# Decay of two tokens from one masked F32 tile, and score tiles placed first in their pool

## The chip, the core and the metric

The kernel runs on one core of a Trainium2 chip. A core has a matrix engine (TensorE, PE in the profile, with its weight loads as PEld), VectorE (DVE), ScalarE (ACT), GpSimd (POOL) and a queue that issues transfers (SyncE, SP). Matrix products write to PSUM, which has eight banks; everything else works on the on-chip memory SBUF, 128 partitions wide. The metric is the device time of one execution in microseconds (us); lower is better. Engines run in parallel and meet only at semaphores, and each engine takes its own instructions in program order.

## What is computed

One layer of a hybrid encoder on 1024 tokens of width 1024, in float32: a mixer made of windowed attention and a bidirectional gated delta rule, then cross-attention into 256 memory tokens, then a gated feed-forward layer. The change lies in the delta rule. For each direction and head, with g the running sum of the per-token log decay, it needs for all pairs of tokens of a chunk

```python
g = jnp.cumsum(g.reshape(b, h, n, c), axis=-1)
incl = jnp.tril(jnp.ones((c, c), dtype=bool))
decay = jnp.exp(jnp.where(incl, g[..., :, None] - g[..., None, :], -jnp.inf))
lower = jnp.where(strict, jnp.einsum('bhnid,bhnjd->bhnij', kb, k) * decay, 0.0)
sol = lax.linalg.triangular_solve(tmat, rhs, left_side=True, lower=True, unit_diagonal=True)
qk = jnp.einsum('bhnid,bhnjd->bhnij', q, k) * decay
```

The second half of the mixer's work that matters here is the windowed attention: scores of a block of 128 tokens against itself and its neighbours, a softmax with a sink, and the product with the values.

## The kernel before, in words

The kernel works in chunks of 128 tokens, eight in all. Matrix products that must be precise in float32 are made of two faster ones: an operand x is split into a high part, x rounded to the type F32R, and a low part, the rest (`split`, L99 to L106), and products of the parts are added in PSUM. A product of two plain F32 tiles is also possible; the kernel uses it for small ones.

The mixer runs in three stretches, each written as a list of steps (ORDER_1 to ORDER_3, L36 to L38), but the order in which an engine issues its instructions is not the order of that list: a scheduler works out every engine's order from the program's dependences and priorities when the kernel is built. Any edit can therefore move instructions that it does not name.

Stretch one, ORDER_1. For each of four heads, D projects and convolves k, q and v (`proj`, products L259; `conv`, four VectorE steps per tile, L284), and P prepares (`prep`, L431): it makes the decay of all token pairs, E; transposes k, q and v (L441), norms them (sums on ACT, L463; rs on POOL, L159 and L160; the product kv on VectorE, L466), transposes back (L473), forms k with k and q with k (L481), and multiplies both with E (U at L484, pc at L488). B inverts the 32x32 diagonal blocks of two heads at a time (`base_inverse`, L498) on VectorE (L515 to L528), with A at L529 on POOL; V and A then go to DRAM (d_inv, L533). B0 serves heads 0 and 1, called group 0, B1 heads 2 and 3, group 1.

E is the exponential of a sum that PE forms in PSUM. With a mask tile mi (ones where token s is at or before token t, or after it for the other direction) times the log decays G of one head, and a triangular matrix ml as the other operand, one product gives the decay sum of every pair of tokens of four chunks at once. G is first split: `ghr` is G cast to F32R, `ghi` its value and `glo` the rest (L352 to L357). For each head, half of the sequence and direction, POOL makes one masked tile `gm` of the high part and one of the low part, and PE adds the four products of both directions in one PSUM bank (L445 to L452). The masked tiles rotate through two buffers, so POOL writes the third when PE has read the first.

Stretch two, ORDER_2. L (`levels`, L536) builds the inverse of each head's whole chunk from the diagonal blocks: it fetches them from d_inv into cz and cw (L544), rearranges them (m5, c5, c6 at L554 to L557; D and Z at L567), masks the transposed U (L5, L6 at L575 and L576), and runs two levels of products (L583 and L589), whose results Z (L605, L606) go to DRAM. G, A and V project the gate, the attention's q and k with their rotary products (sn and rop, L724 and L725), and the values; the values are transposed (L741) and split into `vhl` (L743). W runs the attention windows (`window`, L612), which write their scores into tiles `sc`. Stretch three, ORDER_3, runs the recurrent scan over chunks (L777) with the rest of the windows and the projections of the memory; then the merge product (L1005) begins.

Memory is handed out by pools, which are laid on a stack in the order in which they open. A pool that opens after another closed takes over its memory, and the first instruction that writes a tile there waits until every reader and writer of the old tiles on that spot is done, transfers included. Between stretches one and two the pools of `base_inverse` (tb) and of `prep` (t2) close, and the pool of the windows (tw, L712) opens on the same spot. In a pool each tag's buffers are laid out when it is first asked for; the first here is vhl, 9,216 bytes a partition, and the eight score tiles of 1,536 bytes come later. The inverse's pool held V and A of 4,096 bytes, two small tiles of 128 and tmpb of 1,024.

Of the kernel before, what the change touches and what calls it, by code (L numbers as in the profile page):

```python
# [10 lines left out]
F32 = mybir.dt.float32  # L11
F32R = mybir.dt.float32r
I32 = mybir.dt.int32
AF = mybir.ActivationFunctionType
ALU = mybir.AluOpType
# [4 lines left out]
P = 128  # L20
# [3 lines left out]
NT = S // P  # L24
# [51 lines left out]
def tile_hybrid_block(  # L76
# [6 lines left out]
    nc = tc.nc  # L83
# [9 lines left out]
    def f32(ap):  # L93
        return ap.bitcast(F32)

    def bc(ap, axis, shape):
        return ap.unsqueeze(axis).to_broadcast(list(shape))
# [10 lines left out]
    def pool(name, bufs, **kw):  # L108
        return tc.tile_pool(name=name, bufs=bufs, reuse_waits="tile", **kw)
# [27 lines left out]
    sm = p12.enter_context(pool("sm", 1))  # L137
    C0, C1 = _AT["mUi"], _AT["mU"]
    C = sm.tile([P, C1 - C0], F32, name="C")
    mU_r = sm.tile([P, P], F32R, name="mU_r")  # L140
    mL_r = sm.tile([P, P], F32R, name="mL_r")
    prm = sm.tile([P, 24], F32, name="prm")
    nega = sm.tile([P, 8], F32, name="nega")
    p1 = ExitStack()
# [8 lines left out]
    cm = {n: (C[:, a - C0:a - C0 + P] if a < C1 else CE[:, a - C1:a - C1 + P]) for n, a in _AT.items() if n != "ident"}  # L153
    rope_f, rope_s = (CE[:, _ROPE_AT - C1 + i:_ROPE_AT - C1 + i + 1] for i in range(2))

    def rstd_of(rs, ss, n, eps):

        w = ss.shape[-1]
        nc.gpsimd.tensor_scalar(rs, ss, n, eps, ALU.mult, ALU.add)  # L159
        nc.gpsimd.tensor_tensor(rs, rs, mhalf[:, :w], ALU.pow)  # L160
# [33 lines left out]
    t1 = pa1.enter_context(pool("t1a", 2, side="right"))  # L194

    def small():
        return ps.tile([P, 512], F32, tag="ps", name="ps")
# [11 lines left out]
    for hf in range(2):  # L209
        hi = hx.tile([P, KT, HALF], F32R, name=f"hhi{hf}")  # L210
        lo = hx.tile([P, KT, HALF], F32R, name=f"hlo{hf}")
        for j in range(4):
# [10 lines left out]
            for kq in range(2):  # L223
                pt = small()
                for k in range(4):
                    c = (4 * kq + k) * P
# [15 lines left out]
    nc.scalar.copy(cols, pt[:, :P])  # L242
    nc.sync.dma_start(CE, consts[:, C1:])
    nc.sync.dma_start(C, consts[:, C0:C1])
    nc.vector.tensor_copy(mU_r, cm["mU"])
    nc.vector.tensor_copy(mL_r, cm["mL"])

    nc.sync.dma_start(prm[:, 0:8], a_log[0].rearrange("d h -> (d h)").partition_broadcast(P))
    nc.sync.dma_start(prm[:, 8:16], dt_bias[0].rearrange("d h -> (d h)").partition_broadcast(P))
# [21 lines left out]
    t2 = pp_.enter_context(pool("t2", 2))  # L271
# [28 lines left out]
    t1 = pa1.enter_context(pool("t1b", 1, side="right"))  # L300
# [8 lines left out]
    for hf in range(2):  # L309
        pp = pg.tile([P, 512], F32, tag="pg", name="pg")  # L310
        for k in range(KT):
            for a in range(2):
                nc.tensor.matmul(pp, wabr[:, k, :], hT[hf][a][:, k, :], start=(k == 0 and a == 0),
                                 stop=(k == KT - 1 and a == 1))
# [27 lines left out]
    G = sm.tile([P, 2, 4, NT], F32, name="G")  # L342
# [6 lines left out]
    dump("G", G)  # L349
    dump("beta", beta)  # L350

    ghi = sm.tile([P, 2, 4, NT], F32, name="ghi")  # L352
    glo = sm.tile([P, 2, 4, NT], F32, name="glo")
    ghr = t1.tile([P, 2, 4, NT], F32R, tag="ghr", name="ghr")
    nc.vector.tensor_copy(ghr, G)
    nc.vector.tensor_copy(ghi, f32(ghr))
    nc.vector.tensor_tensor(glo, G, ghi, ALU.subtract)  # L357

    pt = small()
    pv = pt[:, 0:192].rearrange("p (s d n) -> p s d n", s=3, d=2)  # L360
# [54 lines left out]
    def together(gens):  # L415

        gens = list(gens)
        while gens:
            gens = [g for g in gens if next(g, g) is not g]
# [3 lines left out]
    def save(after=None):  # L423

        while unsaved:
            with ExitStack() as order_:
                if after:
                    order_.enter_context(tc.issue_after(after.ins))
                nc.sync.dma_start(*unsaved.pop(0))

    def prep(h, kc, qc, vc):  # L431

        g, hh = h // 2, h % 2
        def part(b):
            c4 = slice(4 * b, 4 * b + 4)

            def turned(src):
                p_ = small()
                for j in range(4):
                    o = (4 * b + j) * P  # L440
                    nc.tensor.transpose(p_[:, j * P:(j + 1) * P], src[:, o:o + P], ident)  # L441
                return p_.rearrange("p (c n) -> p c n", c=4)


            pa = small()  # L445
            n = 0
            for d, (mi, ml) in enumerate((("mUi", mL_r), ("mLi", mU_r))):
                for part in (ghi, glo):
                    gm = t2.tile([P, 4, P], F32R, tag="gm", name="gm")
                    nc.gpsimd.tensor_tensor(gm, bc(part[:, d, h, c4], 2, (P, 4, P)), bc(cm[mi], 1, (P, 4, P)), ALU.mult)  # L450
                    nc.tensor.matmul(pa, ml, gm.rearrange("p c n -> p (c n)"), start=(n == 0), stop=(n == 3))
                    n += 1  # L452
            E = t2.tile([P, 4, P], F32, tag="E", name="E")
            nc.scalar.activation(E, pa.rearrange("p (c n) -> p c n", c=4), AF.Exp)

            kv = t2.tile([P, 4, 4, P], F32, tag="kv", name="kv")
            for src, i, n, e in ((kc, 0, 1.0, EPS), (qc, 3, float(P), P * EPS)):
                yield
                pk = turned(src)
                ss = t2.tile([P, 4], F32, tag="ss4", name="ss4", bufs=4)  # L460
                for j in range(4):
                    jk = t2.tile([P, P], F32, tag="jk", name="jk")
                    nc.scalar.activation(jk, pk[:, j, :], AF.Square, accum_out=ss[:, j:j + 1])  # L463
                rs = t2.tile([P, 4], F32, tag="rs4", name="rs4", bufs=4)
                rstd_of(rs, ss, n, e)
                nc.vector.tensor_tensor(kv[:, :, i, :], pk, bc(rs, 2, (P, 4, P)), ALU.mult)  # L466
            yield
            nc.scalar.copy(kv[:, :, 1, :], turned(vc))
            for i, o in ((0, 2), (3, 3)):
                yield  # L470
                p_ = small()
                for j in range(4):
                    nc.tensor.transpose(p_[:, j * P:(j + 1) * P], kv[:, j, i, :], ident)  # L473
                nc.scalar.copy(kv[:, :, o, :], p_.rearrange("p (c n) -> p c n", c=4))
            nc.sync.dma_start(d_kv[g][c4, :, hh].rearrange("c p s n -> p c s n"), kv)

            for i in (2, 3):
                yield
                p_ = small().rearrange("p (c n) -> p c n", c=4)
                for j in range(4):  # L480
                    nc.tensor.matmul(p_[:, j, :], kv[:, j, 2, :], kv[:, j, i, :], start=True, stop=True)  # L481
                if i == 2:
                    U = t2.tile([P, 4, P], F32, tag="U", name="U")
                    nc.vector.tensor_tensor(U, p_, E, ALU.mult)  # L484
                    nc.sync.dma_start(d_u[g][hh, c4].rearrange("c p n -> p c n"), U)
                else:
                    pc = t2.tile([P, 4, P], F32, tag="pc", name="pc")
                    nc.vector.tensor_tensor(pc, p_, E, ALU.mult)  # L488
                    for d, mi in enumerate(("mUi", "mLi")):
                        pm = t2.tile([P, 4, P], F32, tag="pm", name="pm", bufs=3)  # L490
                        nc.gpsimd.tensor_tensor(pm, pc, bc(cm[mi], 1, (P, 4, P)), ALU.mult)
                        unsaved.append((d_pz[g][d][c4, :, hh, 0].rearrange("c p n -> p c n"), pm))
            if h < 3:
                save()

        together([part(b) for b in range(2)])

    def base_inverse(g):  # L498
# [211 lines left out]
    pw = p12.enter_context(pool("pw", 2, space=PSUM, side="right"))  # L710
    ps = pgs.enter_context(pool("psl", 2, space=PSUM))
    tw = p12.enter_context(pool("tw", 2))  # L712
    vhl = tw.tile([P, NT + 1, 2, 2, 64], F32R, tag="vhl", name="vhl", bufs=1)[:, 0:NT]
    tl_ = p1.enter_context(pool("tl", 2))

# [437 lines left out]
    for k in range(HK):  # L1153
        p0, p1 = turned_k(xn, k), turned_k(xn, k + HK)
        g0, g1 = gain("ffn", k), gain("ffn", k + HK)
        x12, t1, t2_, t3_ = (tr.tile([P, HALF], F32, name=f"r{i}", tag=f"r{i}") for i in range(4))
# [352 lines left out]
```

## Time and profile before

| | us |
|---|---|
| median of 3 runs | 1587.42 |
| lowest and highest run | 1584.72, 1590.94 |
| the profiled execution, its own time | 1588.8 |
| its span, first to last instruction | 1587.1 |
| mean granted PE clock in it | 0.988 |

The profile is of one execution. Its page gives busy time by engine, the span in slices, and the chain of work that ended last, followed back from the end. The trace behind it can be asked for windows of time, for the waits of one engine, for a tile, or for the instructions in order of time. A row of the last kind reads: start in us from the span's start, duration, engine, line, operation, output<-inputs, shape, count, and in brackets how long the engine stood idle just before and which work released it. Matrix products are pipelined: the duration of one is a latency, and what it costs the engine is the distance to the next start.

### The profile page before, as it was taken

How to read it: one execution, taken by the hardware profiler on the slowest of the kernel's cores; microseconds unless marked ns; L12 is line 12 of the kernel's file. 1: busy time of each engine (PE TensorE's matmuls, PEld its weight loads, DVE VectorE, ACT ScalarE, POOL GpSimd, SP SyncE). 2: the span in 40 equal slices, each digit the busy share in tenths (PEclk: the TensorE clock that was granted, in tenths of full speed). 3: DMA queues.
4: the chain of work that ended last, by engine and by line, in shares of the span. 5: the costliest groups of instructions: out<-in, count | busy, mean ns of one | idle time of the engine just before them, and what ended most of it. 6: DMA issues, size and time to landing. Idle time of an engine off the chain costs nothing.

```text
span 1587.1 us, 21186 instructions
## 1 busy us (share of the span) xinstructions
PE 1505.9 (95%) x7514; PEld 1260.3 (79%) x7514; DVE 1059.3 (67%) x1616; ACT 762.4 (48%) x1523; POOL 497.4 (31%) x447
## 2 busy tenths in 40 slices
PE   6999889989799989999999999999999999999998
PEld 5877777868689967788888777888888888888786
DVE  6846887975678865444345549677768655596565
ACT  6556543238766685554335566322322332344532
POOL 2368644233134510243301140443434433100021
PEclk9999999989999999999999999999999999999999
DMA  6134148483998675455222254443335332853354
GB/s 207 42 118 129 41 153 226 113 206 103 283 289 284 191 251 206 146 186 157 69 72 79 90 186 140 128 154 127 118 118 166 100 100 100 292 206 112 107 171 161
DMA packets 252151, 242.97 MB, mean 153 GB/s; under 512 B 33528, under 2 KB 187021, under 8 KB 252045
## 3 DMA queue, kind: packets, MB, share of 16 engines
q1 hardware_dynamic: 252045, 241.62, 48.0%
q8 instruction: 59, 0.97, 0.3%
q14 instruction: 47, 0.39, 0.1%
HBM read 172.07 MB, written 66.88 MB: 151 GB/s over the span
## 4 chain that ended last, share of the span: by engine, by line
PE 67%; DVE 13%; DMA 7%; ACT 5%; issue 3%; POOL 3%; SPq 2%; DVEq 0%; POOLq 0%; ACTq 0%
PE pmg L1005 8%; PE pD L1180 7%; PE pE L1180 7%; PE pA L1180 6%; PE pcq L259 6%; PE pdX L1370 5%; PE pg L259 4%; PE pdA L1370 4%; PE pB L1180 4%; PE psc L777 3%; DVE acc L284 2%; PE pdD L1370 2%; DVE tmpb L524 2%; DVE A L526 2%; PE pcs L1086 1%
## 5 line engine op out<-in xcount | busy, mean ns | idle before, releaser
L102 ACT CAST whi<-wraw 128x1024 fp32r<-128x1024 f32 x108 | 113.3, 1050 | 161.5 <-PE pmg L1005 34.9
L103 POOL TENSOR_TENSOR wlo<-wraw,whi 128x1024 fp32r<-128x1024 f32 x48 | 119.7, 2494 | 193.9 <-ACT whi L102 171.4
L259 PE MATMUL pg<-hlo,whi 128*128 128x512 f32 x352 | 140.2, 399 | 0.0
L259 PE MATMUL pg<-hhi,whi 128*128 128x512 f32 x352 | 140.1, 399 | 0.1
L259 PE MATMUL pg<-hhi,wlo 128*128 128x512 f32 x352 | 139.9, 398 | 0.0
L103 DVE TENSOR_TENSOR wlo<-wraw,whi 128x1024 fp32r<-128x1024 f32 x60 | 74.5, 1244 | 79.4 <-ACT whi L102 75.1
L1005 PE MATMUL pmg<-whi,b 128*128 128x512 f32 x384 | 118.4, 394 | 2.6 <-ACT whi L102 2.2
L1180 PE MATMUL pA<-s,whi 128*128 128x512 f32 x352 | 109.6, 392 | 1.4 <-ACT m L1197 1.4
L284 DVE SCALAR_TENSOR_TENSOR acc<-cp,cols,acc 128x1024 f32<-128x1024 f32 x48 | 73.8, 1539 | 19.5 <-ACT acc L282 18.9
L1005 PEld LDWEIGHTS pmg<-whi,b 128*128 128x128 f32 x384 | 71.2, 188 | 17.9 <-ACT whi L102 2.7
L259 PEld LDWEIGHTS pg<-hhi,whi 128*128 128x128 f32 x352 | 67.1, 191 | 13.6 <-ACT hhi L102 0.4
L1257 POOL TENSOR_TENSOR act<-act,up 128x512 f32<-128x512 f32 x33 | 50.1, 1519 | 88.1 <-DVE up L1256 53.0
L259 PEld LDWEIGHTS pg<-hhi,wlo 128*128 128x128 f32 x352 | 67.1, 191 | 13.2
L259 PEld LDWEIGHTS pg<-hlo,whi 128*128 128x128 f32 x352 | 67.2, 191 | 13.1
L1370 PE MATMUL pdX<-dhl,whi 128*128 128x512 f32 x264 | 76.1, 390 | 1.5 <-ACT dhl L102 0.8
L1180 PEld LDWEIGHTS pA<-s,whi 128*128 128x128 f32 x352 | 65.3, 188 | 15.2 <-ACT m L1197 2.0
L1400 POOL TENSOR_SCALAR frs<-sq 128x1 f32<-128x1 f32 x8 | 11.9, 1497 | 195.7 <-ACT jk L1389 194.8
L1005 PE MATMUL pmg<-wlo,b 128*128 128x512 f32 x192 | 71.4, 391 | 0.0
L1180 PE MATMUL pA<-s,wlo 128*128 128x512 f32 x176 | 68.8, 392 | 1.9 <-DVE wlo L103 1.9
L102 ACT CAST whi<-araw 128x1024 fp32r<-128x1024 f32 (+1 forms) x36 | 35.4, 982 | 71.3 <-PE pdX L1370 27.6
L1229 POOL TENSOR_TENSOR sr<-wraw 128x512 f32<-128x512 f32 x22 | 29.2, 1328 | 126.4 <-DMA wraw<-in_w_gate_up_dram 125.6
L103 DVE TENSOR_TENSOR wlo<-araw,whi 128x1024 fp32r<-128x1024 f32 (+1 forms) x36 | 40.7, 1132 | 38.5 <-ACT whi L102 38.3
(409 smaller groups left out, 4230.3 us busy)
## 6 DMA issues: line engine op xcount, KB each, us to landing
wraw<-in_w_gate_up_dram SPq DMA_DIRECT2D x52, 512.0 KB, 3.9
kv<-d_kv SPq DMA_DIRECT2D x32, 512.0 KB, 6.7
wraw<-in_w_in_dram SPq DMA_DIRECT2D x22, 512.0 KB, 4.3
b<-in_w_down_dram SPq DMA_DIRECT2D x20, 512.0 KB, 7.0
araw<-d_as SPq DMA_DIRECT2D x20, 512.0 KB, 3.7
d_kv<-kv SPq DMA_DIRECT2D x8, 1024.0 KB, 7.2
pz<-d_pz SPq DMA_DIRECT2D x32, 256.0 KB, 6.0
wraw<-in_w_ckv_dram SPq DMA_DIRECT2D x16, 512.0 KB, 7.2
```

What stands on the lines that cost most here:

```text
L102: nc.scalar.copy(hi, src)
L103: (eng or nc.vector).tensor_tensor(lo, src, f32(hi), ALU.subtract)
L259: nc.tensor.matmul(p_, w[:, k, :], ah[a][:, k, :], start=(k == 0 and i == 0), stop=(k == nk - 1 and i == 2))
L284: nc.vector.scalar_tensor_tensor(acc, cp[:, t:t + S], taps[t], acc, ALU.mult, ALU.add)
L524: nc.vector.tensor_tensor(tv, A[:, j + 1:, j:j + 1].to_broadcast([P, n, j]), A[:, j:j + 1, 0:j].to_broadcast([P, n, j]), ALU.mult)
L526: nc.vector.tensor_tensor(A[:, j + 1:, 0:j], A[:, j + 1:, 0:j], tv, ALU.add)
L777: nc.tensor.matmul(out[:, d, h, :], lt[:, d, h, :], rt[:, d, h, :], start=True, stop=True)
L1005: nc.tensor.matmul(pp[t], act[a][:, k, tt], w_[:, kk, :], start=(k == 0 and i == 0), stop=(k == KT - 1 and i == 2))
L1180: nc.tensor.matmul(out_, w[a][:, k, :], xx[b_][:, k, :], start=(start and k == 0 and i == 0), stop=(k == HK - 1 and i == 2), skip_group_ch ...
L1229: nc.gpsimd.tensor_tensor(s[0], b_[:, 0:HK], b_[:, HK:], ALU.add)
L1257: nc.gpsimd.tensor_tensor(o_, o_, up, ALU.mult)
L1370: nc.tensor.matmul(banks[t], a[:, k - k0, tt], w, start=(first and k == 0 and i == 0), stop=(k == NB - 1 and i == 2), skip_group_check=not ...
```

## The change

The split of G into ghr, ghi and glo is gone. For each direction one masked tile of G itself is made, in F32, and one product in F32 is added; the two triangular operands are kept as F32 copies, mU_s and mL_s, instead of F32R ones. So a head needs four masked tiles and four products where it needed eight of each. And in the pool of the windows a score tile is asked for first, so that the eight buffers of that tag are laid at the pool's start, ahead of vhl; the tile that this line returns is not used.

```diff
-    mU_r = sm.tile([P, P], F32R, name="mU_r")
-    mL_r = sm.tile([P, P], F32R, name="mL_r")
+    mU_s = sm.tile([P, P], F32, name="mU_s")
+    mL_s = sm.tile([P, P], F32, name="mL_s")
...
-    nc.vector.tensor_copy(mU_r, cm["mU"])
-    nc.vector.tensor_copy(mL_r, cm["mL"])
+    nc.vector.tensor_copy(mU_s, cm["mU"])
+    nc.vector.tensor_copy(mL_s, cm["mL"])
...
-    ghi = sm.tile([P, 2, 4, NT], F32, name="ghi")
-    glo = sm.tile([P, 2, 4, NT], F32, name="glo")
-    ghr = t1.tile([P, 2, 4, NT], F32R, tag="ghr", name="ghr")
-    nc.vector.tensor_copy(ghr, G)
-    nc.vector.tensor_copy(ghi, f32(ghr))
-    nc.vector.tensor_tensor(glo, G, ghi, ALU.subtract)
...
-            n = 0
-            for d, (mi, ml) in enumerate((("mUi", mL_r), ("mLi", mU_r))):
-                for part in (ghi, glo):
-                    gm = t2.tile([P, 4, P], F32R, tag="gm", name="gm")
-                    nc.gpsimd.tensor_tensor(gm, bc(part[:, d, h, c4], 2, (P, 4, P)), bc(cm[mi], 1, (P, 4, P)), ALU.mult)
-                    nc.tensor.matmul(pa, ml, gm.rearrange("p c n -> p (c n)"), start=(n == 0), stop=(n == 3))
-                    n += 1
+            for d, (mi, ml) in enumerate((("mUi", mL_s), ("mLi", mU_s))):
+                gm = t2.tile([P, 4, P], F32, tag="gm", name="gm")
+                nc.gpsimd.tensor_tensor(gm, bc(G[:, d, h, c4], 2, (P, 4, P)), bc(cm[mi], 1, (P, 4, P)), ALU.mult)
+                nc.tensor.matmul(pa, ml, gm.rearrange("p c n -> p (c n)"), start=(d == 0), stop=(d == 1))
...
     tw = p12.enter_context(pool("tw", 2))
+    tw.tile([P, 384], F32, tag="sc", name="sc", bufs=8)
     vhl = tw.tile([P, NT + 1, 2, 2, 64], F32R, tag="vhl", name="vhl", bufs=1)[:, 0:NT]
```

## The prediction, made before the result was known

> **What bounds the kernel now.** I read the page's busy shares and its chain first.
>
> ```profile
> span 1587.1 us, 21186 instructions
> PE 1505.9 (95%) x7514; PEld 1260.3 (79%) x7514; DVE 1059.3 (67%) x1616; ACT 762.4 (48%) x1523; POOL 497.4 (31%) x447
> PE 67%; DVE 13%; DMA 7%; ACT 5%; issue 3%; POOL 3%; SPq 2%; DVEq 0%; POOLq 0%; ACTq 0%
> ```
>
> PE is busy for 95% of the span and is two thirds of the chain. POOL, which loses most work in this change, is 3% of the chain. Such averages decide nothing for one stage, so next come windows of 20 us over the mixer. Columns: window, its length, busy time of PE, PEld, DVE, ACT, POOL, then granted clock, DMA share, GB/s.
>
> ```profile
> 140.00:160.00 20.00, 19.25 (x109) 16.37 (x108) 10.09 (x11) 7.99 (x13) 12.21 (x14) 1.00 0.67 204
> 180.00:200.00 20.00, 15.38 (x78) 12.65 (x77) 19.52 (x32) 14.74 (x44) 10.50 (x13) 0.91 0.11 30
> 220.00:240.00 20.00, 15.58 (x78) 12.70 (x77) 14.66 (x22) 13.23 (x43) 9.60 (x12) 0.93 0.43 107
> 320.00:340.00 20.00, 14.43 (x72) 11.59 (x71) 15.51 (x18) 6.30 (x14) 9.93 (x7) 0.99 0.90 211
> 340.00:360.00 20.00, 18.16 (x90) 16.27 (x91) 16.18 (x38) 9.77 (x23) 5.64 (x5) 0.75 0.70 185
> 360.00:380.00 20.00, 20.00 (x119) 17.69 (x119) 12.39 (x28) 16.23 (x39) 10.36 (x8) 1.00 0.52 158
> ```
>
> PE is full in 140:160 and 360:380 and stands for about 5 us in each of 180:200, 220:240 and 320:340; in 340:360 it also has three quarters of its clock. So the mixer is PE's work plus a few holes. The view of waits says who dug them (PE, first 640 us; total, times, longest).
>
> ```profile
> PE ps L441 <- DVE kv L466: 5.5, 3, 2.6
> PE ps L583 <- DVE L L576: 5.0, 1, 5.0
> PE ps L473 <- DVE kv L466: 3.8, 3, 1.7
> PE ps L451 <- POOL gm L450: 2.9, 3, 1.5
> PE ps L574 <- DVE Z L606: 2.4, 1, 2.4
> PE ps L441 <- ACT E L454: 2.0, 1, 2.0
> ```
>
> Two families: four lines around the decay (L451, E, and the kv that waits for rs in POOL's queue), 14.2 us in sum, and two in the levels of head 2 (L574, L583), 7.4 us. The change touches both. From the merge product (L1005) on, the two built programs issue the same order on every engine, so the whole effect lies ahead of it and shifts the rest.
>
> **Term 1, PE passes: a loss.** The 32 F32R products of L451 become 16 F32 products of the same 128x512 shape.
>
> ```profile
> L451 PE MATMUL ps<-gm,mL_r x16: 387/395/499, 71.1 to 221.8; 128*128 128x512 f32 x16
> 33.56 13.85 PE pg L259 x61
> 529.34 1.79 PE psc L777 x16
> L777 PE MATMUL psc<-kv,pz 128*128 128x128 f32 x128 | 19.1, 284 | 2.3 <-DMA pz<-d_pz 2.0 <-DVE kv L798 0.3
> ```
>
> The 395 ns is latency; what PE pays is the step in the chain: 61 F32R products of 512 columns in 13.85 us, 0.227 each, so 32 cost 7.3 us. Of F32 the trace has only narrow ones. L777 issues 64 such products with kv and pz (4 per call, 8 steps, 2 groups) and leaves 128 records, two per product, while L451 in F32R leaves one (16 for mL_r). A record of 128 columns steps at 1.79/16 = 0.112. If columns scale, one F32 product of 512 columns is 2 x 4 x 0.112 = 0.90 and 16 are 14.3, a loss of 7.0 us. If each record is no dearer than an F32R one, 32 records cost 7.3 and the loss is 0. I take 7.0: the F32 row is the nearest in kind.
>
> The Trainium skill, "FP8 and Floating Point Precision", section TensorE Precision Notes, speaks against the change: true FP32 takes four passes through the array. By it 16 products are 64 passes of 0.227, 14.5 us, a loss of 7.2; no row of before shows a wide F32 product.
>
> Where these 7 us lie: in the new order the decay does not push the chain back, since 642 projection matmuls stand ahead of the last product of head 3 (L481) where 673 stood, and 895 where 935 stood ahead of the first L583 of head 2. The 40 deferred ones (9.1 us) come later, in a stretch like 360:380 where PE has no hole. So the loss is paid at the end of the projections, before the scan.
>
> **Term 2, fewer masks on POOL: a gain.** Sixteen of 32 gm go, and three 128x64 VectorE steps (the dearest 0.82).
>
> ```profile
> L450 POOL TENSOR_TENSOR gm<-ghi,C x16: 1033/1120/2023, 68.2 to 226.8; 128x512 fp32r<-128x512 f32 x16
> L450 POOL TENSOR_TENSOR gm<-glo,C x16: 1034/1089/2089, 69.4 to 227.8; 128x512 fp32r<-128x512 f32 x16
> 68.46 0.82 DVE L357 TENSOR_TENSOR glo<-G,ghi 128x64 f32<-128x64 f32 x1
> 227.87 0.50 PE L451 MATMUL ps<-gm,mU_r 128*128 128x512 f32 x1 [1.54 <-POOL gm L450]
> 229.19 2.12 DVE L528 TENSOR_TENSOR V<-A,bB 128x1024 f32<-128x1024 f32 x1
> 231.39 2.75 POOL L529 TENSOR_TENSOR A<-A,bB 128x1024 f32<-128x1024 f32 x1 [2.58 <-DVE V L528]
> 235.81 0.69 DVE L466 TENSOR_TENSOR kv<-ps,rs 128x512 f32<-128x512 f32 x1 [3.45 <-POOL rs L160]
> 236.65 0.63 PE L441 MATMUL ps<-ident,acc 128*128 128x128 f32 x4 [2.54 <-DVE kv L466]
> ```
>
> At a median of 1.1 us that is 17.6 us of POOL time, nearly all beside PE work and worth nothing there. On PE's path it can be worth from 0 to the 14.2 us of the four waits. I take half of the 2.9 (gm) and 2.0 (E), since each tile has half as many masks before it, and a quarter of the 9.3 (kv): its rs stands in POOL's queue behind gm at some heads, and at head 3 behind A of the inverse, which stays. Together 2.5 + 2.3 = 4.8, say 5.
>
> **Term 3, score tiles first: a gain.** Before, the first tile of its pool, vhl (9,216 bytes a partition), lies on the memory of the inverse's V and A. With eight score tiles in front (12,288 bytes, the inverse's pool had 9,472) it lies on tiles of the decay stage, long free, and both vhl copies lose their DMA waits. The score tiles inherit the old memory, but are first written by the windows, after those stores.
>
> ```profile
> 288.68 0.28 PE L741 MATMUL ptv<-ident,vT 128*128 128x128 f32 x1
> 317.73 2.04 DVE L528 TENSOR_TENSOR V<-A,bB 128x1024 f32<-128x1024 f32 x1
> 322.23 1.18 SPq L533 DMA_DIRECT2D d_inv<-A  x2
> 326.42 1.07 ACT L102 CAST vhl<-ptv 128x512 fp32r<-128x512 f32 x2 [10.07 <-DMA d_inv<-A]
> 327.05 1.29 DVE L103 TENSOR_TENSOR vhl<-ptv,vhl 128x512 fp32r<-128x512 f32 x2 [4.20 <-ACT vhl L102]
> 328.33 0.65 ACT L605 ACTIVATE Z<-ps 64x256 f32<-64x256 f32 x2
> 330.23 1.09 PE L574 MATMUL ps<-ident,Ul 128*128 128x128 f32 x8 [2.37 <-DVE Z L606]
> 331.75 4.18 DVE L555 COPY c<-cw 32x256 f32<-32x256 f32 x4
> 341.84 3.59 PE L583 MATMUL ps<-m,L 128*128 128x32 f32 x16 [5.04 <-DVE L L576]
> 358.92 1.73 PE ps L583 x16
> ```
>
> The data of vhl are ready at 289; ACT holds it until A has landed, 10.07 us of idle time. Behind it stand khi and the two Z copies (L605) that free the two PSUM banks PE needs for L574, and VectorE idles 4.20 us; its c, D and L steps then end late and PE waits again at L583. In the new order the Z copies stand ahead of vhl on both engines, so the 2.37 goes. What stands ahead of vhl instead is a c copy that waits for a cw fetch, which follows V's store, not A's; behind it wait vhl, khi and the next weight cast. On SP that fetch waits for V's store and the stores of A and of Z queue behind it. So the start of head 2's levels still hangs on the inverse: of the 5.04 I take the 4.20 that VectorE idled. After the hole 16 records of L583 took 3.59 instead of 1.73, and the window had clock 0.75, a loss of at most 0.25 x 20 = 5.0; I take 1.5. Term 3: 2.4 + 4.2 + 1.5 = 8.1; bounds 0 and 2.4 + 5.0 + 5.0 = 12.4.
>
> **Sum.** +7.0 - 4.8 - 8.1 = -5.9. The profiled execution took 1588.8 us (span 1587.1), 1.4 over the median of 1587.42, so 1582.9 for it and 1581.5 for the median.
>
> **Rivals.** One, *the holes swallow the passes*: the F32 records run where PE stands anyway, and term 1 costs nothing. For: PE has some 5 us of hole in each of three windows. Against: the deferred projections fall into full windows. -12.9, 1574.5; with all of term 3's bound, about 1570.
>
> Two, *the wait moves*: ACT stands as long at the c copy as it stood at vhl, because V's store and fetch in SP's queue come no sooner. Term 3 is 0: +7.0 - 4.8 = +2.2, 1589.6. For: nothing shortens the inverse itself. Against: VectorE reaches its start with 22 weight splits and no rotary products ahead where 23 and 4 stood.
>
> Three, slower, *head 3's masks behind the inverse of group 0*: the new POOL order puts A<-A,bB ahead of the last two masks of head 3, which stood ahead of it. PE takes L451 in order, so the projections behind it wait for V, A (2.75) and two masks (2.2): a hole of 5.0, and everything of head 3 and group 1 starts later, which eats terms 2 and 3. +7.0 + 5.0 = +12.0, 1599.4. It decides where V ends after PE has come to these masks; before, PE came at 227.87 and V began at 229.19, so it is close. Against it: 44 convolution steps stand ahead of that V where 48 stood:
>
> ```profile
> L284 DVE SCALAR_TENSOR_TENSOR acc<-cp,cols,acc 128x1024 f32<-128x1024 f32 x48 | 73.8, 1539 | 19.5 <-ACT acc L282 18.9
> ```
>
> Four of 1.539 us are 6.2 us earlier.
>
> **Chances.** Forecast 0.42 (its own range 1575 to 1588), rival one 0.20, two 0.18, three 0.20. The range goes from rival one with most of its bound to three: 1566 to 1600. A measurement of this kernel tells about 0.5%, 8 us, from no change, so faster means under 1579.5: rival one and half of the forecast, 0.41. Slower means over 1595.4: rival three and a tail of two, 0.22. The rest, 0.37, is within.
>
> **What would show it.** Right: L451 in 32 records whose step is near 0.45; vhl with no DMA as releaser and well before the inverse's A lands; no 2.4 us hole at L574, a smaller one at the first L583 of head 2; the scan's first product some 6 us earlier than here:
>
> ```profile
> 408.51 1.20 PE L777 MATMUL psc<-kv,pz 128*128 128x128 f32 x4 [1.97 <-DMA pz<-d_pz]
> ```
>
> Wrong: L451 records stepping at 0.23 (term 1 too dear); ACT idle about 10 us at the c copy before vhl (two); a hole over 4 us at L451 near 225 with POOL's A as cause (three). A first scan product later than this row would make the sum's sign wrong.

## The result, and the profile after

The changed kernel took 1589.53 us in the median of 20 runs (1586.75 to 1595.8), the kernel before 1587.01 us in as many beside it. The ratio is 1.0020, 95% interval 1.0012 to 1.0028: about 3 us slower, where the forecast had it 6 us faster. The difference is below the 8 us that the forecast called "within", but the whole interval lies above 1. The page of the profiled execution:

```profile
span 1587.5 us, 21156 instructions
PE 1511.1 (95%) x7514; PEld 1258.4 (79%) x7514; DVE 1058.5 (67%) x1613; ACT 756.2 (48%) x1519; POOL 466.5 (29%) x431
```

PE is busy 5.2 us longer than before, POOL 31 us shorter, and the span is the same within what one execution tells.

In the changed kernel L441 is L435 and L451 is L443; lines from 454 to about 704 are 9 lower (L574 is L565, L583 is L574, L528 is L519), and later ones 8 (L777 is L769). First the products of the decay, from the view of one line (count, shortest/median/longest in ns, first and last start) and from the timeline:

```profile
L443 PE MATMUL ps<-gm,mL_s x16: 590/591/1203, 71.3 to 223.3; 128*128 128x512 f32 x16
L443 PE MATMUL ps<-gm,mU_s x16: 592/592/1062, 72.2 to 225.7; 128*128 128x512 f32 x16
160.51 1.02 PE L443 MATMUL ps<-gm,mL_s 128*128 128x512 f32 x2
161.37 1.02 PE L443 MATMUL ps<-gm,mU_s 128*128 128x512 f32 x2
```

Sixteen products leave 32 records. Two records start 0.86 us ahead of the next two, so a product costs 0.86, not 0.90, and sixteen cost 13.8: 6.5 more than the 7.3 of before. By the Trainium skill, "FP8 and Floating Point Precision", section TensorE Precision Notes, true FP32 takes four passes; 64 passes of 0.227 make an estimate of 14.5 us, and the trace agrees within 5%.

The waits of PE in the first 640 us (total, times, longest):

```profile
PE ps L435 <- ACT E L445: 5.4, 3, 3.8
PE ps L574 <- DVE L L567: 4.2, 4, 1.8
PE ps L443 <- POOL gm L442: 4.1, 1, 4.1
PE ps L464 <- DVE kv L457: 3.7, 7, 1.1
PE ps L574 <- ACT m L545: 3.6, 1, 3.6
PE ps L565 <- DVE Z L597: 1.9, 1, 1.9
```

The four lines around the decay stood at 14.2 us and are now three with 5.4 + 4.1 + 3.7 = 13.2. The levels stood at 7.4; now the L583 wait of 5.0 in one piece is 4.2 in four, the 2.4 is 1.9, and a new one of 3.6 behind ACT's copy m has come: 9.7. In the same windows as before:

```profile
140.00:160.00 20.00, 20.00 (x106) 17.17 (x105) 10.30 (x9) 6.70 (x9) 8.88 (x8) 1.00 0.76 235
180.00:200.00 20.00, 19.11 (x106) 16.31 (x107) 18.18 (x31) 11.68 (x35) 7.75 (x10) 0.91 0.47 159
220.00:240.00 20.00, 15.53 (x72) 11.05 (x73) 9.51 (x9) 13.19 (x44) 9.04 (x11) 0.91 0.48 110
320.00:340.00 20.00, 16.42 (x75) 13.79 (x74) 15.84 (x20) 5.89 (x11) 8.59 (x6) 0.88 0.88 213
340.00:360.00 20.00, 20.00 (x115) 17.62 (x114) 14.12 (x33) 11.80 (x32) 5.72 (x7) 0.95 0.65 155
360.00:380.00 20.00, 17.55 (x87) 14.69 (x86) 12.70 (x25) 9.21 (x23) 11.02 (x9) 0.91 0.62 186
```

The hole in 180:200 has nearly closed, 320:340 has 2 us more of PE at a lower clock (0.88 for 0.99), and 340:360 is full at 0.95 where it had 0.75. But 220:240 is no better, and 360:380, which was full, now has a hole of 2.5. Head 3's masks show where 220:240 went (POOL, then PE):

```profile
217.54 2.74 POOL L520 TENSOR_TENSOR A<-A,bB 128x1024 f32<-128x1024 f32 x1 [5.19 <-DVE V L519]
220.24 4.00 POOL L442 TENSOR_TENSOR gm<-G,C 128x512 f32<-128x512 f32 x2
222.31 2.06 PE L443 MATMUL ps<-gm,mL_s 128*128 128x512 f32 x2 [4.13 <-POOL gm L442]
```

A of the inverse stands ahead of the two masks, and PE waits 4.13 us for the first of them: the mechanism of rival three. Then the levels of head 2, on ACT, on SP's queue and on PE:

```profile
322.84 0.40 ACT L548 COPY c<-cw 64x256 f32<-64x256 f32 x1 [5.58 <-DMA cw<-d_inv]
323.26 1.07 ACT L102 CAST vhl<-ptv 128x512 fp32r<-128x512 f32 x2
331.93 0.82 ACT L545 COPY m<-cz 32x256 f32<-32x256 f32 x2 [5.57 <-DMA cz<-d_inv]
```

```profile
320.22 1.26 SPq L524 DMA_DIRECT2D d_inv<-A  x2
321.57 3.92 SPq L599 DMA_DIRECT2D d_pz<-Z  x4
325.58 3.44 SPq L721 DMA_DIRECT2D rot<-sn  x4
329.06 0.58 SPq L535 DMA_DIRECT2D cz<-d_inv  x1
```

```profile
334.58 3.27 PE L574 MATMUL ps<-m,L 128*128 128x32 f32 x16 [3.58 <-ACT m L545]
411.12 1.06 PE L769 MATMUL psc<-kv,pz 128*128 128x128 f32 x4
```

The copy to vhl no longer waits for a DMA. But ACT idles 5.58 us at the c copy ahead of it and 5.57 at the m copy behind it, 11.2 in sum where it idled 10.07 once. The fetch of cz stands in SP's queue behind four stores and four rotary copies and leaves at 329.06; before, it left 3.2 us sooner though V ended 3 us later (319.77 against 316.67):

```profile
325.87 0.53 SPq L544 DMA_DIRECT2D cz<-d_inv  x1
```

The scan's first product came at 411.12, 2.6 us later than before: the row that the forecast named for a wrong sign. The delay does not last in these two traces, though. The first merge product (L1005, now L997) starts at 600.51 where before it started at 602.90, and the spans differ by 0.4 us. The 3 us are those of the medians; one execution of each kernel does not show where they arise.

### The profile page after: what moved, and what is told of

It reads as the page before. It is cut to its first block, busy times and chain, and to the rows that moved or that the text cites. A ratio compares the mean times of both kernels' runs of the same rounds, so it can differ in the third digit from the quotient of the medians.

```text
span 1587.5 us, 21156 instructions
## 1 busy us (share of the span) xinstructions
PE 1511.1 (95%) x7514; PEld 1258.4 (79%) x7514; DVE 1058.5 (67%) x1613; ACT 756.2 (48%) x1519; POOL 466.5 (29%) x431
## 5 line engine op out<-in xcount | busy, mean ns | idle before, releaser
L997 PE MATMUL pmg<-whi,b 128*128 128x512 f32 x384 | 118.4, 394 | 2.6 <-ACT whi L102 2.2
L997 PEld LDWEIGHTS pmg<-whi,b 128*128 128x128 f32 x384 | 71.2, 188 | 17.9 <-ACT whi L102 2.7
L284 DVE SCALAR_TENSOR_TENSOR acc<-cp,cols,acc 128x1024 f32<-128x1024 f32 x48 | 77.5, 1616 | 9.4 <-ACT acc L282 8.5
L259 PEld LDWEIGHTS pg<-hlo,whi 128*128 128x128 f32 x352 | 67.4, 192 | 13.7 <-issue 1.0
L997 PE MATMUL pmg<-wlo,b 128*128 128x512 f32 x192 | 71.4, 391 | 0.0
```

What stands on the lines that cost most here:

```text
L259: nc.tensor.matmul(p_, w[:, k, :], ah[a][:, k, :], start=(k == 0 and i == 0), stop=(k == nk - 1 and i == 2))
L284: nc.vector.scalar_tensor_tensor(acc, cp[:, t:t + S], taps[t], acc, ALU.mult, ALU.add)
L997: nc.tensor.matmul(pp[t], act[a][:, k, tt], w_[:, kk, :], start=(k == 0 and i == 0), stop=(k == KT - 1 and i == 2))
```

## The experiments

Each ratio is to the kernel before, run beside it on the same chip; medians are of 5 to 20 runs. Differences between two runs are given in us of 1587, and their uncertainties are estimates from the two intervals.

| run | median us | ratio | 95% interval |
|---|---|---|---|
| changed kernel | 1589.53 | 1.0020 | 1.0012 to 1.0028 |
| p1_f32_alone | 1590.83 | 1.0029 | 1.0016 to 1.0042 |
| p2_sc_first_alone | 1587.21 | 0.9998 | 0.9990 to 1.0007 |
| r16_one_tile_f32r | 1581.69 | 0.9966 | 0.9955 to 0.9978 |
| f32_32_products | 1600.14 | 1.0078 | 1.0066 to 1.0090 |
| gm4_four_masks | 1596.36 | 1.0060 | 1.0045 to 1.0076 |
| zf_fetch_ahead | 1590.47 | 1.0026 | 1.0014 to 1.0039 |
| zg_both | 1599.27 | 1.0079 | 1.0062 to 1.0097 |
| pzg_both_hi_lo | 1599.33 | 1.0077 | 1.0059 to 1.0094 |
| am_masks_then_A | 1593.26 | 1.0032 | 1.0019 to 1.0045 |
| m16_masks_halved | 1585.40 | 0.9987 | 0.9977 to 0.9997 |
| r16n_no_score_tile | 1584.63 | 0.9986 | 0.9974 to 0.9997 |
| i15_half_inverse | 1584.24 | 0.9983 | 0.9972 to 0.9994 |

Two things are read from the traces first. Three pairs issue the same instructions in the same order on every engine, and differ in the placement alone: the kernel before and p2_sc_first_alone, p1_f32_alone and the changed kernel, r16n_no_score_tile and r16_one_tile_f32r. The edits of the decay, in type, number of masks or buffers, move instructions on every engine within the first 150 us, so what they cost or return includes another order. And where the order is the same up to the second inverse, its V ends at 316.67 in the changed kernel, at 318.92 in p1_f32_alone and at 319.71 in zf_fetch_ahead: start times of single traces tell nothing below some 3 us.

**The two parts alone.** First the changed kernel without its score-tile line.

```diff
-    tw.tile([P, 384], F32, tag="sc", name="sc", bufs=8)
```

> The F32 tile alone: the decay from one masked tile in F32, vhl left where it lay in the kernel before. Theory (each part has its own sign): the passes add 16 x 2 x 0.45 - 32 x 0.227 = 7.1 us of PE work, and up to 320 us the changed kernel had the same lost PE time as before (45.3 against 45.2), so the mixer's decay stage gives nothing back: +7 us against before, ratio 1.0044, with ACT still standing about 10 us at vhl for A. Rival one (the passes run in holes): ratio 1.000 +- 0.001. Rival two (all of the 2.5 us by which the changed kernel is slower come from this part, the placement does nothing): +2.5 us, ratio 1.0016.

Measured 1.0029, +4.6 us: between the theory's +7, which lies outside the interval, and the second rival's +2.5 at its edge. This is terms 1 and 2 without term 3. The part on ACT did not come:

```profile
324.89 0.40 ACT L548 COPY c<-cw 64x256 f32<-64x256 f32 x1 [4.32 <-DMA cw<-d_inv]
327.50 1.07 ACT L102 CAST vhl<-ptv 128x512 fp32r<-128x512 f32 x2 [2.21 <-DMA d_inv<-A]
334.38 0.82 ACT L545 COPY m<-cz 32x256 f32<-32x256 f32 x2 [3.77 <-DMA cz<-d_inv]
```

With the order of the changed decay the c copy stands ahead of vhl and waits for the same inverse, so vhl itself waits only 2.21 us, and the placement has no more than that to take there. The changed kernel, which is this run with the placement, is 1.4 us faster, uncertain by 2.4. Then the kernel before with the score-tile line and nothing else.

```diff
+    tw.tile([P, 384], F32, tag="sc", name="sc", bufs=8)
     vhl = tw.tile([P, NT + 1, 2, 2, 64], F32R, tag="vhl", ...
```

> The placement alone: score tiles first in their pool, the decay left in high and low parts in F32R. Theory (each part has its own sign): the lost PE time of the changed kernel after 320 us is about 6 us smaller than before (45.1 against 51.3 up to 650 us), so -4 to -6 us, ratio 0.9962 to 0.9975; vhl without a DMA wait, ACT idle 5 us at the c copy and 5 us at the m copy of head 2 instead of 10 us once. Rival (the wait only moves): ratio 1.000 +- 0.001. Rival (a new hole behind the moved work): ratio above 1.001.

Measured 0.9998: the placement is worth nothing here, at most 1.6 us. The theory of -4 to -6 falls. ACT and PE in this run:

```profile
316.30 1.08 ACT L102 CAST vhl<-ptv 128x512 fp32r<-128x512 f32 x2
328.33 0.82 ACT L554 COPY m<-cz 32x256 f32<-32x256 f32 x2 [6.68 <-DMA cz<-d_inv]
338.65 3.59 PE L583 MATMUL ps<-m,L 128*128 128x32 f32 x16 [4.41 <-ACT c L557]
343.48 0.63 PE L259 MATMUL pg<-hhi,whi 128*128 128x512 f32 x1
```

vhl is written 10 us earlier and waits for nothing, exactly as meant. ACT then runs out of other work and stands 6.68 us at m, for the same inverse. The hole at L583 is 4.41 where it was 5.04, the same 16 records take the same 3.59 us, and the projections behind still run slowly (0.63 us of latency against 0.39). The 2.37 us at L574 did go: its eight records start at 327.75 without a wait. But the scan's first product starts at 408.35, with 2.85 us of waiting for pz, where it was 408.51 with 1.97: by then nothing of the gain is left.

**The price of the passes.** One masked tile in F32R:

```diff
-    mU_s = sm.tile([P, P], F32, name="mU_s")
+    mU_s = sm.tile([P, P], F32R, name="mU_s")
...
-                gm = t2.tile([P, 4, P], F32, tag="gm", name="gm")
+                gm = t2.tile([P, 4, P], F32R, tag="gm", name="gm")
```

> The changed kernel with the masked tile and both triangles in F32R, so that the low part of G is left out of the decay: 16 one-record products in place of 16 two-record ones. 16 x 0.227 = 3.6 us of PE in place of 14.3, 10.7 less than the changed kernel. Theory (PE's passes are paid in full): -10 us against the changed kernel, about -8 against before, ratio 0.995. Rival one (the passes run in holes): as the changed kernel, ratio 1.0016. Half paid would give -5 against the changed kernel, ratio 0.9985.

Measured 0.9966. Against the changed kernel that is 0.0054, 8.6 us, for 16 x (0.86 - 0.227) = 10.1 us of PE work. That would be most of it, but the order differs and PE's waits with it: for head 3's masks it waits 0.5 us here and 4.1 in the changed kernel, for E 1.6 and 5.4. And the other way, the placement alone with F32 in its 32 products (mU_r, mL_r and gm declared F32):

> The placement with high and low parts kept, but masked tiles and triangles in F32: 32 two-record products, 28.7 us of PE where the kernel with the placement alone has 7.3. Theory (passes paid in full): +21 us against the placement alone, about +16 against before, ratio 1.010. Rival (the passes run in holes): +5 or less against the placement alone. The step of two records should be 0.43 to 0.45 us a record as in the changed kernel.

Measured 1.0078, 12.7 us over the placement alone, for 32 x (0.86 - 0.227) = 20.3 us of PE work: neither in full nor hidden. Then masks without passes:

```diff
+                for n in range(2):
+                    nc.tensor.matmul(pa, ml, gm..., start=(d == n == 0), stop=(d == n == 1))
...
-            nc.scalar.activation(E, ..., AF.Exp)
+            nc.scalar.activation(E, ..., AF.Exp, scale=0.5)
```

> Masks halved without PE's part: 16 masked tiles in F32R, each multiplied twice and the sum halved in the exponential, so 32 F32R products as before; the low part of G is left out. PE's work is that of the kernel before; 16 masks (17.6 us of POOL) and three VectorE steps are gone. Theory (masks are worth about 2 us: the run with one F32R tile was 5.4 us under before, of which 3.6 are PE's products): -1 to -3 us, ratio 0.998 to 0.9995. Rival one (the forecast's term 2): -4.8, ratio 0.997. Rival two (the masks were beside PE work and worth nothing): 1.000, and then the 5.4 us came from PE's products alone.

Measured 0.9987, as the theory had it: -2.1 us against before, and rival one's 0.997 lies outside the interval. Against the placement alone it is 0.0011, 1.7 us, uncertain by 2.1, so that the masks are worth something beside it is not shown. The changed kernel has as many masks and 6.5 us more of PE's products, and stands 0.0033 above: 5.2 us, uncertain by 2.0. The order of the two differs on PE from 78 us on, so these 5.2 us are not the products' alone. So far 5.2 of 6.5 us of PE work, 8.6 of 10.1 and 12.7 of 20.3 came out in the time, 80, 85 and 63%; whether the share falls with the amount can't be told from three runs that differ in order too.

**The holes taken away.** Four buffers for the masked tile (`gm = t2.tile(..., bufs=4)`):

> The changed kernel with four buffers for the masked tile instead of two; in the program's POOL order the last masks of head 3 then stand ahead of A<-A,bB of group 0 again. Theory (the new order's hole of 4.13 us at L443 and of 3.8 us at E's products are its own loss, and they come from the masks' place): L443 waits under 1 us on POOL, E's wait under 2, together 5 to 7 us less hole, ratio to before 0.997 to 0.999 where the changed kernel has 1.0016. Rival (the hole only moves to the next wait on the inverse): L443 without a wait but the ratio stays 1.001 to 1.002.

Measured 1.0060, 6 us slower than the changed kernel, which neither side expected. Its waits, from the same view as above:

```profile
PE ps L435 <- ACT E L445: 7.8, 3, 5.1
PE ps L435 <- ACT acc L285: 5.9, 2, 3.5
```

L443 no longer waits, but the buffers changed the order of every head's decay, and PE waits for the exponential and for the convolutions instead, 13.7 us in sum. As a test of the one hole it was too coarse; a finer one is below. Next the SP queue: the Z stores of head 1 are kept back until head 2 has issued its fetches, and those get a higher priority.

```diff
+                if h == 2:
+                    early.enter_context(tc.high_priority(AHEAD))
                 fetch(cz[d], 1, d)
                 fetch(cw[d], 0, d)
+        save()
...
-                nc.sync.dma_start(d_pz[...], Z[d])
+                unsaved.append((d_pz[...], Z[d]))
+            if h != 1:
+                save()
```

> The changed kernel with the fetches of head 2's levels ahead of the Z stores of head 1 and of most of the rotary copies in SP's queue. Theory (the start of the levels hangs on SP's queue: cz waited there from 321.5 to 329.1 behind four Z stores, 3.92 us, and four copies, 3.44): ACT's idle time at the m copy falls from 5.6 to under 2, the first L574 of head 2 comes 4 to 7 us sooner than 334.58, PE's waits there shrink by 3 to 4 us, ratio to before 0.999 to 1.000. Rival (the stretch is held by VectorE's own work, or the next wait takes its place): the fetches come sooner, ratio stays 1.001 to 1.002.

Measured 1.0026. The fetch of cz leaves 4.9 us after V's end where it left 12.4 after it, and the wait of L574 for m is gone. Yet its first product in head 2 starts at 336.53, not 4 to 7 us ahead of 334.58, two c copies on ACT now wait 4.58 and 3.51 us for cw, and the time is that of the changed kernel or a little above. The windows of the changed kernel, then of this run (length and PE busy first):

```profile
320.00:400.00 80.00, 73.97 (x393) 63.79 (x392) 51.34 (x103) 44.14 (x104) 26.81 (x22) 0.94 0.60 160
400.00:500.00 100.00, 91.83 (x677) 83.64 (x676) 79.91 (x208) 68.59 (x159) 28.64 (x26) 0.98 0.95 292
```

```profile
320.00:400.00 80.00, 75.96 (x414) 65.40 (x413) 51.02 (x105) 42.86 (x102) 29.90 (x24) 0.96 0.62 168
400.00:500.00 100.00, 90.24 (x682) 83.07 (x681) 74.94 (x201) 68.10 (x158) 27.86 (x24) 1.00 0.95 290
```

PE is busy 2.0 us longer in the levels and 1.6 less in the scan's first 100 us. Both edits together, on the changed kernel and on the placement alone:

> Both edits on the changed kernel: four masked tiles and the fetches ahead. Theory (both holes are lost time of a full PE): -8 to -11 us against the changed kernel, ratio to before 0.995 to 0.997. Rival (the holes do not decide): 1.001 to 1.002. Between them 0.999: one of the two edits does the work, and which shows in the two runs that make one of them alone.

> Both edits on the kernel with the placement alone, decay in high and low parts in F32R, so 7.1 us less of PE and 16 more masks on POOL than the run with both on the changed kernel. Theory (passes of a full PE are paid, the masks are not): 4 to 7 us under that run, ratio to before 0.991 to 0.994 if that run comes at 0.996. Rival (the masks cost as much as the passes): the same time as that run.

Measured 1.0079 and 1.0077: no gain, and 6.5 us less of PE work made no difference between them, though their order differs too. The second waits for its masks instead, which fits the rival:

```profile
PE ps L451 <- POOL gm L450: 5.8, 5, 4.0
```

The last of this family moves one instruction only: A of the inverse behind head 3's masks.

```diff
-        nc.gpsimd.tensor_tensor(A, A, bc(bB, 2, (P, 32, 32)), ALU.mult)
+        with tc.issue_after(masks[3].ins):
+            nc.gpsimd.tensor_tensor(A, A, bc(bB, 2, (P, 32, 32)), ALU.mult)
```

> The changed kernel with one edge added: POOL issues A<-A,bB of the inverse behind the last masks of head 3. POOL stood 5.19 us ahead of that A, so the two masks have room there; PE's order is the changed kernel's up to there. Theory (the 4.13 us hole at L443 is lost time of its own): L443's wait under 1 us, 3 to 5 us faster than the changed kernel, ratio to before 0.998 to 1.000. Rival (the stretch hangs on the inverse and the hole turns up at the next wait): L443 without a wait, ratio 1.001 to 1.002 as the changed kernel. The run with four masks moved the decay of all heads and says nothing on this hole alone.

Measured 1.0032: the rival. PE and ACT in this run, and below them E and the same transposes in the changed kernel:

```profile
218.68 1.02 PE L443 MATMUL ps<-gm,mL_s 128*128 128x512 f32 x2
231.70 0.69 PE L435 MATMUL ps<-ident,acc 128*128 128x128 f32 x2 [5.75 <-ACT E L445]
227.39 1.28 ACT L285 ACT_TABLE_LOAD   x1 [6.45 <-DVE acc L284]
231.05 0.60 ACT L445 ACTIVATE E<-ps 128x512 f32<-128x512 f32 x1
```

```profile
230.38 0.60 ACT L445 ACTIVATE E<-ps 128x512 f32<-128x512 f32 x1
231.03 0.66 PE L435 MATMUL ps<-ident,acc 128*128 128x128 f32 x4
```

The 4.13 us hole is gone, L443 runs 3.6 us earlier, and PE then stands 5.75 us at its next transposes (L435), 16 projection products further on. These start at 231.70; with the hole they started at 231.03 without a wait. ACT's E is queued behind an activation that waits 6.45 us for a convolution of VectorE, so E comes at 231.05 here and at 230.38 with the hole. So the stretch waits for VectorE, whose queue carries the inverse and the convolutions, and the masks' place only decides where PE stands; the last run below bears this out.

**The placement with a short decay.** The one-tile F32R kernel without the score-tile line:

> One F32R masked tile (low part of G left out) with vhl where it lay in the kernel before. Theory (the placement is worth nothing on either decay): ratio 0.9966 +- 0.001 as with the score tiles first. Rival (the placement is worth something once the decay is short, since the inverse ends earlier): 0.998 or more.

Measured 0.9986, 3 us above the same with it, uncertain by 2.6. ACT in this run, then with the score tiles first:

```profile
315.98 1.08 ACT L102 CAST vhl<-ptv 128x512 fp32r<-128x512 f32 x2 [8.85 <-DMA d_inv<-A]
321.28 0.82 ACT L545 COPY m<-cz 32x256 f32<-32x256 f32 x2 [2.32 <-DMA cz<-d_inv]
```

```profile
311.06 1.05 ACT L102 CAST vhl<-ptv 128x512 fp32r<-128x512 f32 x2
323.13 0.82 ACT L545 COPY m<-cz 32x256 f32<-32x256 f32 x2 [5.53 <-DMA cz<-d_inv]
```

The wait of 8.85 us at vhl goes, and that at m grows from 2.32 to 5.53. The three pairs that differ in the placement alone give 0.3, 1.4 and 3 us, uncertain by 1.4, 2.4 and 2.6. They agree with one another, and the 8.1 of the forecast lies outside all three.

**VectorE relieved.**

```diff
-        for j in range(1, 31):
+        for j in range(1, 16):
```

> The changed kernel with the inverse's loop cut from steps 1 to 30 to steps 1 to 15, so that half of the elimination is left out. The 120 VectorE steps of both groups took 54.3 us (27.5 for tmpb, 26.8 for A); half of them is 13.6 us for each group, and the PE work stays. Theory (head 3's decay and the start of head 2's levels hang on the inverse, so holes that are filled come back at the next thing that waits for it): V, A and the fetches come sooner by about 14 us, PE's waits at E, gm and L574 shrink from 17.3 us in sum to under 9, 6 to 12 us faster than the changed kernel, ratio to before 0.994 to 0.998. Rival (PE's own work sets the mixer's length, holes are noise of the order): under 2 us, ratio 1.000 to 1.002.

Measured 0.9983, 5.9 us below the changed kernel, just short of the 6 to 12 that the theory gave. V ended 26 us sooner for both groups (191.49 for 217.46, 289.97 for 316.67), where 14 were expected. PE's waits in the stages named, and head 3's E with the transposes behind it:

```profile
PE ps L435 <- ACT E L445: 5.4, 3, 3.8
PE ps L574 <- DVE L L567: 4.8, 2, 3.3
```

```profile
224.20 0.60 ACT L445 ACTIVATE E<-ps 128x512 f32<-128x512 f32 x1
224.85 0.66 PE L435 MATMUL ps<-ident,acc 128*128 128x128 f32 x4
```

The waits for gm and for m are gone from the list; those for E and L stayed, so 10.2 of the 17.3 us were left and not under 9. The three waits for E lie at 129.6, 169.3 and 180.4 us, ahead of the steps that are left out, so this run could not touch them. Head 3's E and the transposes behind it come 6.2 us sooner than in the changed kernel. VectorE was busy 28 us less (1030.5 for 1058.5), and the time fell by 6: VectorE is part of what holds the mixer, not all. The order differs here too, from 186 us on.

## Why the forecast went wrong

Two runs split the sum with the same order of issue. p1_f32_alone holds terms 1 and 2: +4.6 us, where the forecast had +2.2. The changed kernel is that run with the placement, term 3, and lies 1.4 us below it, where the forecast had 8.1. Of the 9.1 us between -5.9 and +3.2, term 3 makes 6.7 and the other two together 2.4. (The steps from placement, 0.9998, over half the masks, 0.9987, to F32 products, 1.0020, are -0.3, -1.7 and +5.2 us; they add up by construction, and the last two also change the order.)

- **What bounds the kernel.** The mixer is PE's work plus a few holes, as said: PE is busy 5.2 us longer, and the waits around the decay and the levels went from 21.6 to 22.9 us in sum. That the effect then shifts the rest as a whole is not shown: in the two traces the scan starts 2.6 us later, the first merge product 2.4 earlier and the end comes 0.4 later. The use made of it was wrong: the holes were treated as sums that an edit can take out one by one. When one was taken out (am_masks_then_A, zf_fetch_ahead, the placement alone), PE stood elsewhere.
- **Term 1, +7.0: the work as argued, its effect not isolated.** The records, their number and their step came as argued (6.5 of PE work). The 5.2 us against m16_masks_halved include another order. The first rival, that the holes swallow the passes, does not hold as a whole: 20.3 us of work cost 12.7 in f32_32_products. That a part is swallowed fits the shares of 63 to 85%.
- **Term 2, -4.8: too large.** It took half of two waits and a quarter of a third. The waits fell from 14.2 to 13.2, and halved masks were worth 1.7 us, uncertain by 2.1. Part of the gain went into the 4.13 us hole of rival three, whose place was right. Its condition was not met as stated: V ended at 217.46, before PE came to these masks at 218.18 (before, PE came at 226.33 and V began at 229.19), but A and the first mask still stood between. Its price of 12 us was wrong: am_masks_then_A shows that without this hole the time is no better.
- **Term 3, -8.1: the step that gave the wrong sign.** The forecast said that VectorE's 4.20 us, the 2.4 at L574 and 1.5 of clock would go with vhl's wait. The wait for A did leave vhl, and in the placement alone the 2.4 went too; of the 5.04 at L583 only 0.6 went, and the slow stretch behind it stayed. (The 1.73 us that the forecast set against the 3.59 belong to products of 64 columns; 16 of these with 32 columns take 1.87 at 261.71.) The time returned was 0.3 us there and 1.4 on the changed decay, because the copies to c and m need the same inverse through the same queue: 6.68 us at m there, 5.58 and 5.57 in the changed kernel. On the changed decay vhl had only 2.21 us left to lose. This is rival two's moved wait. The forecast had its argument in hand ("the start of head 2's levels still hangs on the inverse") and took 4.20 of 5.04 all the same. V ended 3 us sooner in the changed kernel's trace, no more than such traces differ among themselves, and the cz fetch left 3.2 us later.
- **Rival two's number was partly luck.** Its sum of +2.2 (1589.6) is close to the measured 1589.53. But the decay cost 4.6 and not 2.2, the placement returned 1.4 and not 0, and ACT stood 5.58 us at the c copy, not 10; the rest came at m.

What stays open: how the 4.6 us of the decay divide into passes, masks and order, and which of VectorE's instructions other than the inverse's hold the rest of the stretch. The fastest kernel here is r16_one_tile_f32r, 0.3% under before, with the lower precision of its decay.

## What to carry to other kernels

Before a wait is booked as a gain, follow the same producer to its next consumers on that engine and on the DMA queue: if another instruction close behind needs the same data, the wait only changes its name. Do the same for a hole of the busiest engine: look at what the next instruction's inputs wait for, and count as gain only the time by which the latest of them comes earlier. Work added to PE, which is busy 95% of the time here, came out in the time at 63 to 85% of its price in three comparisons; the gains set against it were the least certain part of the sum. And compare orders first: a pair of kernels that issue in the same order prices one edit, a pair that does not prices the new order with it.

## What the runs showed of the hardware

An F32 product of 512 columns leaves two records and costs 0.86 us at a granted clock of 1.00 (160 to 163 us of the changed kernel), 3.8 times the 0.227 of F32R; for 128 columns two records cost 0.22, about the same per column. The Trainium skill, "TensorE: Matmul & The Clock Gate", section "Wait — 56ns, not 53.3ns?", has 215.7 ns from start to start of warm products of 512 columns: four such passes make an estimate of 0.863, which the trace meets. The F32R step here is 5% above that one pass.

Behind the hole of 4.13 us the two records of L443 took 2.06 us where they take 1.02, and the granted clock was 0.59 from 222 to 224 us. Behind the hole of 4.41 in p2_sc_first_alone, 16 records of L583 took 3.59 us where they take 1.87 at 261.71 in the kernel before, and the granted clock was 0.53 from 338 to 342. So removing such a hole might return more than itself. In am_masks_then_A, where it went and a later one of 5.75 us came, the total return was still nothing.
